# Second layer's output projection: six heads by seven half-size products, the sums of y kept in DRAM

## The chip, the cores and the metric

One core of a Trainium2 chip runs the whole kernel. The metric is device time in microseconds: the median of several executions. One execution was also profiled; its rows give the times of single instructions. TensorE (PE) multiplies matrices into PSUM banks, VectorE (DVE), ScalarE (ACT) and GpSimd (POOL) work elementwise, and SyncE (SP), ACT and POOL issue DMAs. Each engine works through its own queue in order.

## What is computed

A decoder step of two layers over 1024 prompt tokens and 8 x 4 sample tokens, together 1056 columns of width 1024. The first layer is a gated linear recurrent unit, the second HGRN2 with 8 heads of 128. The change lies in the last line of the second layer, `y @ w_out`:

```
def _hgrn_layer(x, g_norm, w_in, lb, o_gain, w_out, S0):
    xn = _rmsnorm(x, g_norm)
    u = (xn @ w_in).astype(jnp.float32)
    q, f, iv, gate = jnp.split(u, 4, axis=-1)
    ...
    o, S_T = _hgrn2_chunked(q, k, v, log_g, S0)
    o = o * lax.rsqrt(jnp.mean(o * o, axis=-1, keepdims=True) + EPS) * o_gain.reshape(H_B, DV_B).astype(jnp.float32)
    y = (o.reshape(Bsz, T, INNER_B) * jax.nn.silu(gate)).astype(x.dtype)
    return x + y @ w_out, S_T.astype(x.dtype)
```

After it comes only the final RMS norm.

## The kernel before

Everything is kept transposed: 128 rows of the model width on the partitions, tokens along the free dimension. A float32 product is three matmuls (`mm3`, L238 to L243): each operand is split into a high half rounded to the engine's float32r and a low half, the rest, and high x high, high x low and low x high are summed in PSUM. A split costs ACT one copy (the high half) and DVE or POOL one subtraction (the low half).

The second layer runs head by head. For heads 1 to 7, the input projection of two of the head's four matrices at once (128 columns of q and f, or of gate and v) is done by seven products of half size in place of eight (the scheme of Strassen and Winograd): `seven` takes two 128x1024 blocks of weights as a 2x2 matrix of 128x512 pieces, and the activations as a 2x2 matrix whose columns are the two halves of the tokens, of HT = 528 each. Combinations of activations are built once (`build`, `build1`; the tiles `t2`, `t3`, `t4`), those of the weights for each head on POOL (`combine`, four operations; the low half of a weight is made by ACT and an accumulating DMA that POOL issues, `low`, L315). A product has numbers 1 to 7; a string such as "126b74b53" gives their order, and each b is a burst: a piece of the recurrence (`burst1` to `burst4`) of the head before or of the same head. Within a product there are two passes of QT = 264 tokens, each into its own PSUM bank; products 2, 3 and 5 share one pair of banks, products 1, 4, 6 and 7 the other.

Head h's y leaves the recurrence in `gated`, which `burst4` of head h + 1 runs: L1328 multiplies it, transposed by TensorE, into the gate that waits in the row `SG`. For heads 0 to 5 the row is then stored to DRAM, `yd`, L310.

The output projection has two parts. For the first K1 = 5 heads, after the last `seven`, chunks of 352 tokens of `yd` are loaded again and split (`splits`, L1594 and L328), and for each of the eight blocks m of 128 output rows and each of three chunks, 5 x 3 matmuls of 352 columns are summed in a bank and added on DVE to x (L1635). The bursts that finish heads 6 and 7 stand between these products (`SPOTS1`). The second part, the late one, takes the last K2 = 3 heads in three chunks of tokens of 424, 376 and 256 (`OUT`): 8 x 9 matmuls each, DVE adds them to x (L1732), ACT squares x (L1734), POOL sums the squares (L1743). The norm of a chunk is worked out while the next chunk's products run: after three blocks the row sums (`summed`, L277), after six the spread of the result over the partitions (`spread`, L1689), then the multiplications of `finish` (L1709 on DVE) and the stores of y.

The order on every engine is not that of the program: `Flow` collects the operations with their dependences and an assumed cost, plans them by list scheduling, back and forth, and issues each engine's queue in the order found. Only the operations marked main keep their order on PE. A DMA is issued in the same way, by SP, ACT or POOL, at a place in that engine's queue.

Of the kernel before, what the change touches and what calls it, by code (L numbers as in the profile page):

```python
# [14 lines left out]
F32 = mybir.dt.float32  # L15
# [4 lines left out]
ALU = mybir.AluOpType  # L20
# [5 lines left out]
K1 = 5  # L26
NMM = 3
HC = 1
FQ0, FQ, GV = "1267b4b35", "12b675b43", "126b74b53"
SPOTS, SPOTS0, SPOTS1 = (6, 9, 0, 2), (2, 5, -1, -1), (1, 5, 9, 13, 17, 20)  # L30
# [179 lines left out]
def tile_trunk(ctx: ExitStack, tc: tile.TileContext, xT, prm, hc, w0, wg, wo0, w1, wo1, s_in,  # L210
# [85 lines left out]
    with ExitStack() as l0:  # L296
# [603 lines left out]
        yd = [nc.dram_tensor(f"yd_{h}", (128, TOK), F32, kind="Internal").ap() for h in range(H - 2)]  # L900
# [32 lines left out]
    with ExitStack() as l1:  # L933
# [8 lines left out]
        ls2 = [fixed(f"land{i}", [128, CH], F32, p1) for i in range(1)]  # L942
# [22 lines left out]
        for o, n, keys in ((at, 1024, ATK), (ad, 256, [("ad",)]), (as2, 64, [("as", 0), ("as", 1)]),  # L965
                           (ab, 288, [("ab",)])):
            pool(0.3 * n, lambda o=o: G.memset(o, 0.0), (), keys, 3)
        dve(9, lambda: V.memset(ssq, 1.0), (), [("ssq", i) for i in range(3)], 3)
# [342 lines left out]
        def gated(h, s, sk):  # L1311
# [257 lines left out]
        yh, yl = (list(o[:4]) for o in (xh, xl))  # L1569
        flat = {k: o.rearrange("p x j t -> p (x j t)") for k, o in TB.items()}  # L1570
        for k in ((2, 0), (3, 0), (4, 0), (4, 1)):
            yh.append(flat[k][:, :TOK])
            yl.append(flat[k][:, TOK:])
        for k in range(H):
            if k < 4:
                olds = [("x", 1, k, x) for x in range(2)] + [("T", 1, i, k, x) for i in range(2) for x in range(2)]
            else:
                n, i = ((2, 0), (3, 0), (4, 0), (4, 1))[k - 4]
                olds = [("T", n, i, j, x) for j in range(4) for x in range(2)]
# [3 lines left out]

        def splits(k, cs, eng):

            for c in cs:
                if k < H - 2:
                    x, xk = next(land)
                    dma(x, yd[k][:, chunk(c)], (("yd", k),), (xk,), 3)
                    xk = (xk,)  # L1590
                else:
                    x, xk = SG[k][:, chunk(c)], ykeys(k % 2, c * CH, CH)
# [4 lines left out]
        def yparts(c):  # L1597
# [223 lines left out]
```

## Time and profile before

| | us |
|---|---|
| median of 3 runs | 1075.94 (1075.3 to 1076.88) |
| the profiled execution's own time | 1074.84 |
| its span in the trace | 1073.1 |
| last product of `seven` done, first of the output projection starts | 942.65 |
| late part starts | 1023.43 |
| last matmul of the late part done, row sums of the last chunk | 1061.02 |

The times of single rows are us from the start of the span. In a row of the timeline stand start, duration, engine, line, operation, written tile <- read tiles, sizes, count, and in brackets idle time of the engine before it with what ended it. A row of windows gives for a stretch its length, then for each engine the busy time and the number of instructions, the granted clock of TensorE as a share of full speed, the share of the DMA engines' time, and GB/s. The count takes in the one or two instructions that began before the stretch. Durations of matmuls overlap (a matmul of 264 columns lasts 0.28 us but the next starts after 0.12 us), so the price of a matmul is the distance from start to start.

### The profile page before, as it was taken

What the parts mean: (1) busy time and instruction counts of PE and PEld (TensorE: products, weight loads), DVE (VectorE), ACT (ScalarE), POOL (GpSimd) and SP (SyncE); (2) the same over time, 40 slices, a digit from 0 to 9 for tenths busy, and PEclk for the clock granted to TensorE, in tenths of its full rate; (3) what the DMA queues carried; (4) which work ended last, traced back from release to release, by engine and by line L of the source; (5) the groups of instructions that cost most, each with busy time, mean ns of one, the idle gap of its engine ahead of it and who ended that gap; (6) DMA issues with size and microseconds to landing.
All of it is one profiled execution on the core that took longest, in us unless ns stands there. A gap on an engine that the chain in (4) does not pass through costs nothing.

```text
span 1073.1 us, 25672 instructions
## 1 busy us (share of the span) xinstructions
PE 1050.9 (98%) x10020; PEld 1023.3 (95%) x10020; DVE 745.6 (69%) x1481; ACT 663.7 (62%) x1493; POOL 504.5 (47%) x536
## 2 busy tenths in 40 slices
PE   9999999999999999999989999999999999999997
PEld 9999999999999999999989998989999999989996
DVE  7999996887987787274887556556565475674446
ACT  6578656867765964243467685858586767652323
POOL 3425353354543547455454454455455464541544
PEclk9999999999999999999989999999999999999999
DMA  9111112124832785373675564746465657555204
GB/s 302 60 28 43 56 48 72 58 60 127 270 104 67 217 258 168 108 242 121 188 200 110 130 140 100 178 93 156 89 151 112 155 112 169 140 161 166 84 1 162
DMA packets 92490, 139.59 MB, mean 130 GB/s; under 512 B 11344, under 2 KB 60496, under 8 KB 92368
## 3 DMA queue, kind: packets, MB, share of 16 engines
q1 hardware_dynamic: 75952, 109.49, 31.8%
q0 software_dynamic: 14112, 25.70, 14.3%
q10 hardware_dynamic: 2304, 2.77, 0.8%
q8 instruction: 78, 1.28, 0.5%
q14 instruction: 44, 0.36, 0.1%
HBM read 77.54 MB, written 29.81 MB: 100 GB/s over the span
## 4 chain that ended last, share of the span: by engine, by line
PE 86%; DVE 9%; DMA 3%; issue 1%; ACT 1%; POOL 0%; POOLq 0%; ACTq 0%; SPq 0%; DVEq 0%
PE mm L241 24%; PE mm L242 24%; PE mm L243 23%; PE hg L1057 2%; PE hg L1166 2%; DMA a<-xn 1%; PE hg L1274 1%; PE hg L572 1%; DVE R L1039 1%; PE hg L1276 1%; PE hg L241 1%; PE hg L242 1%; PE hg L243 1%; PE hg L1220 1%; DVE a L1240 1%
## 5 line engine op out<-in xcount | busy, mean ns | idle before, releaser
L241 PE MATMUL mm<-xh,whi 128*128 128x352 f32 (+1 forms) x1111 | 346.6, 312 | 5.7 <-DVE sg L1510 5.7
L242 PE MATMUL mm<-xl,whi 128*128 128x352 f32 (+1 forms) x1111 | 340.7, 307 | 0.0
L243 PE MATMUL mm<-xh,wlo 128*128 128x352 f32 (+1 forms) x1111 | 340.6, 307 | 0.0
L241 PEld LDWEIGHTS mm<-xh,whi 128*128 128x128 f32 x1111 | 209.0, 188 | 8.3 <-DVE sg L1510 6.8
L242 PEld LDWEIGHTS mm<-xl,whi 128*128 128x128 f32 x1111 | 209.3, 188 | 1.5
L243 PEld LDWEIGHTS mm<-xh,wlo 128*128 128x128 f32 x1111 | 209.1, 188 | 0.0
L328 POOL TENSOR_TENSOR wlo<-wraw,whi 128x512 fp32r<-128x512 f32 (+1 forms) x72 | 96.3, 1347 | 105.7 <-ACT whi L383 97.2
L241 PE MATMUL mm<-t,whi 128*128 128x264 f32 (+1 forms) x354 | 104.0, 294 | 0.0
L243 PE MATMUL mm<-t,wlo 128*128 128x264 f32 (+1 forms) x354 | 101.8, 288 | 2.0 <-DMA wlo<-wraw 2.0
L242 PE MATMUL mm<-t,whi 128*128 128x264 f32 (+1 forms) x354 | 101.9, 288 | 0.0
L504 DVE SCALAR_TENSOR_TENSOR k<-xb,prm_sb,k 128x352 f32<-128x352 f32 (+2 forms) x144 | 90.0, 636 | 11.0 <-ACT k L501 6.3
L315 POOL DMA_DIRECT2D wlo<-wraw x59 | 51.6, 888 | 65.6 <-ACT wlo L314 46.6
L1510 DVE TENSOR_TENSOR k<-mm,k 128x264 f32<-128x264 f32 x72 | 30.7, 430 | 62.2 <-PE mm L243 59.4
L243 PEld LDWEIGHTS mm<-t,wlo 128*128 128x128 f32 x354 | 67.2, 190 | 2.3 <-DMA wlo<-wraw 2.3
L241 PEld LDWEIGHTS mm<-t,whi 128*128 128x128 f32 x354 | 67.5, 191 | 0.5 <-ACT k L1487 0.2
L242 PEld LDWEIGHTS mm<-t,whi 128*128 128x128 f32 x354 | 67.5, 191 | 0.0
L587 POOL TENSOR_TENSOR k<-X 128x352 f32<-128x352 f32 x36 | 42.8, 1198 | 47.8 <-DVE R L588 38.6
L383 ACT CAST whi<-wraw 128x512 fp32r<-128x512 f32 (+2 forms) x75 | 41.3, 569 | 31.3 <-PE mm L242 19.8
L315 POOL DMA_DIRECT2D wlo<-R x36 | 33.5, 929 | 49.7 <-ACT wlo L314 48.2
L241 PE MATMUL mm<-yh,whi 128*128 128x352 f32 x153 | 49.9, 326 | 0.0
L243 PE MATMUL mm<-yh,wlo 128*128 128x352 f32 x153 | 49.4, 323 | 0.0
L242 PE MATMUL mm<-yl,whi 128*128 128x352 f32 x153 | 49.4, 323 | 0.0
(422 smaller groups left out, 2742.1 us busy)
## 6 DMA issues: line engine op xcount, KB each, us to landing
wraw<-in_w_dram SPq DMA_DIRECT2D x88, 256.0 KB, 3.1
wlo<-wraw POOLq DMA_DIRECT2D x59, 256.0 KB, 4.1
wlo<-R POOLq DMA_DIRECT2D x36, 256.0 KB, 4.0
wraw<-in_wo_dram SPq DMA_DIRECT2D x34, 192.0 KB, 2.5
si<-in_s_in_dram SPq DMA_DIRECT2D x8, 512.0 KB, 4.5
R<-in_w_dram SPq DMA_DIRECT2D x16, 256.0 KB, 3.8
out_ss_out_dram<-si SPq DMA_DIRECT2D x8, 512.0 KB, 2.6
sg<-x1b SPq DMA_DIRECT2D x21, 176.0 KB, 3.1
```

What stands on the lines that cost most here:

```text
L241: T.matmul(out, wh, xh, start=first, stop=False, skip_group_check=chained)
L242: T.matmul(out, wh, xl, start=False, stop=False, skip_group_check=chained)
L243: T.matmul(out, wl, xh, start=False, stop=last, skip_group_check=chained)
L315: fl.add("POOL", 0.93, lambda: G.dma_start(dst.bitcast(F32), src, accum_op=ALU.add), (*r, *w), w, prio, n / 2)
L328: emit = lambda: e.tensor_tensor(b, x, a.bitcast(F32), op=ALU.subtract)
L383: act(m, lambda hi=hi, raw=raw, m=m: S.copy(hi[:, :m], raw[:, :m]), rk, (hk,), prio)
L504: dve(u, lambda src=src, dst=dst, sh=sh, k=k: V.scalar_tensor_tensor(dst, sh(src, k), pc("cw", 12 * k + m), dst, op0=ALU.mult, op1=ALU.add ...
L572: fl.add("PE", 0.62, lambda ps=ps, i=i, c=c: T.matmul(ps[:96, :CH], gs[:, i, :], ST[:96, chunk(c)], start=True, stop=True), (("gs",), *((" ...
L587: pool(CH, lambda x=x, a=a, b=b: G.tensor_tensor(x, a.bitcast(F32), b.bitcast(F32), op=ALU.add), (ak, bk), (xk,), 3)
L1057: T.matmul(ps[32 * j:32 * j + 32, n * w:n * w + w], B[:, o:o + 32], q(slice(o, o + 32)), start=True, stop=True, tile_position=(0, 32 * j))
L1166: T.transpose(ps[:, n * 128:(n + 1) * 128], row[:, a:a + 128], ident)
L1510: dve(QT, lambda: V.tensor_tensor(o[0], z[0], u[0], op=ALU.add), (z[1], u[1]), (o[1],), 0)
```

## The change

K1 becomes 6, K2 becomes 2. The first six heads are multiplied by the scheme of seven products, with three heads each as the two rows of the 2x2 matrix: head h and head h + 3 pair up (j = h mod 3), blocks m and m + 1 of the output are the two rows of the weights, the two halves of the tokens the columns. Instead of storing y, `gated` stores what the seven products need of it. `ysum` in DRAM has seven places for each j; a head's two halves are written or added to several of them: for heads 0 to 2 two plain stores (four places at once, then one) and one accumulating store of three places, for heads 3 to 5 two plain stores of one place and accumulating stores of three places and of one. Signs are dealt with by `hogn`, the negative of the gain, for which L1328 is cut at token 528. The accumulating stores are issued by POOL, and each waits until the earlier stores to the same places have landed.

`youts` loads the seven operands (three pieces of 528 tokens each) into the places from which the last `seven` reads its own, as each comes free, and splits them: one piece on DVE, two on POOL. `seven_out` then does the products, for four pairs of blocks: 7 x 2 passes x 3 x 3 matmuls of 264 columns for each pair. Its weights, pieces of 128x384, are combined and their low halves subtracted on POOL, 11 operations for each pair. Each pass is added to x2 by DVE, 264 columns at a time. The orders of products and bursts are in `LAST`. The late part keeps its shape with two heads in place of three.

```diff
-K1 = 5
+K1 = 6
...
-SPOTS, SPOTS0, SPOTS1 = (6, 9, 0, 2), (2, 5, -1, -1), (1, 5, 9, 13, 17, 20)
+SPOTS, SPOTS0 = (6, 9, 0, 2), (2, 5, -1, -1)
+LAST = "12b675b43", "126b74b53", "12b675b43", "1267543"
...
             for ps, pk, a, n in got:
-                w = SG[h][:, a:a + n]
-                dve(n, lambda ps=ps, w=w: V.scalar_tensor_tensor(w, ps, hog[:, h:h + 1], w, op0=ALU.mult, op1=ALU.mult),
-                    (pk,), ykeys(h % 2, a, n), 3)
-            if h < H - 2:
-                dma(yd[h], SG[h], ykeys(h % 2, 0, TOK), (("yd", h),), 4, 528)
+                for u, v in [(0, min(n, HT - a)), (HT - a, n)] if h < K1 and a < HT < a + n else [(0, n)]:
+                    w, z = SG[h][:, a + u:a + v], ps[:, u:v]
+                    by = hogn if h < K1 and (h < 3) == (a + u >= HT) else hog
+                    dve(v - u, lambda z=z, w=w, by=by: V.scalar_tensor_tensor(w, z, by[:, h:h + 1], w, op0=ALU.mult, op1=ALU.mult),
+                        (pk, ("hogn",)), ykeys(h % 2, a + u, v - u), 3)
+            if h < K1:
+                j, first, second = h % 3, (SG[h][:, :HT], ykeys(h % 2, 0, HT)), (SG[h][:, HT:], ykeys(h % 2, HT, HT))
+                for add, (x, xk), a, b in ((False, first, 0, 4), (False, second, 4, 5), (True, second, 1, 4)) if h < 3 else \
+                        ((False, first, 5, 6), (False, second, 6, 7), (True, second, 2, 5), (True, first, 3, 4)):
+                    y, x, keys = ysum[j, :, a:b, :], x[:, None, :].to_broadcast([128, b - a, HT]), [("ysum", p, j) for p in range(a, b)]
+                    if add:
+                        fl.add("POOL", 0.93, lambda y=y, x=x: G.dma_start(y, x, accum_op=ALU.add), (*xk, *keys), keys, 4, 264 * (b - a))
+                    else:
+                        dma(y, x, xk, keys, 4, 264 * (b - a))
...
+        def youts(p):
...
+            for (hi, lo), j, m in pieces:
+                src, sk = ysum[j, :, place_of[p], :], ("ysum", place_of[p], j)
...
+                dma(lo.bitcast(F32), src, (sk,), (lk,), 2, 264)
+                act(HT, lambda hi=hi, lo=lo: S.copy(hi, lo.bitcast(F32)), (lk,), (hk,), 2)
+                subtract(YSUB[j], HT, lo, lo.bitcast(F32), hi, (hk, lk), (lk,), 2)
...
+        YSUB = V, G, G
...
+        def seven_out(m, order, at):
...
+            def split(p):
+                (raw, rk), (hi, hk), (lo, lk) = slot[named[p]], next(his), next(los)
+                hi, lo = hi[:, :u], lo[:, :u]
+                act(u, lambda: S.copy(hi, raw), (rk,), (hk,), 2)
+                subtract(V if p in BYDVE else G, u, lo, raw, hi, (rk, hk), (lk,), 2)
...
+            combine("s", "21", "22", ALU.add)
+            combine("21", "11", "21", ALU.subtract)
+            combine("11", "s", "11", ALU.subtract)
+            combine("12", "11", "12", ALU.subtract)
...
+                for x in range(2):
+                    ps, pk = chains[p in (2, 3, 5)][x]
+                    new = p in (1, 2, 5) or apart and p == 3
+                    ops = [(a[:, x * QT:x * QT + QT], b[:, x * QT:x * QT + QT], k) for a, b, k in youtput[p]]
+
+                    def emit(ps=ps, ops=ops, hi=hi, lo=lo, new=new):
+                        for j, (uh, ul, _) in enumerate(ops):
+                            w = slice(128 * j, 128 * j + 128)
+                            mm3(ps[:, :QT], (hi[:, w], lo[:, w]), uh, ul, new and j == 0, j == 2, True)
+
+                    pe(1.09, emit, (*wk, *(k for o in ops for k in o[2])), (pk,))
...
+                    if p == 1:
+                        add(m, first, z, ALU.add)
...
-        for n, (m, c) in enumerate([(m, c) for c in range(NCH) for m in range(2)] + [(m, c) for m in range(2, KD) for c in range(NCH)]):
...
-            ps, pk = product(ws2[m], yparts(c), 8 if m > 1 else 1)
-            dve(CH, lambda x=x, ps=ps: V.tensor_tensor(x, ps[:, :CH], x, op=ALU.add), (pk, *xk), xk, 0)
+        for i, order in enumerate(LAST):
+            seven_out(2 * i, order, ends_[2 * i:2 * i + 2])
```

The queues move at three places. The first is POOL's where the last of the six heads' y is handed over (during `seven` of head 7). `wlo` is the low half of a weight, `gp` a small copy for the recurrence. Before:

```order
L1437 TENSOR_TENSOR wraw<-wraw,R 128x512
L1437 TENSOR_TENSOR R<-R,wraw 128x512
L315 DMA wlo<-wraw 128x512 x2
L1050 COPY gp<-sg 128x8
L315 DMA wlo<-wraw 128x512
```

and now:

```order
L1449 TENSOR_TENSOR wraw<-wraw,R 128x512
L1341 DMA ysum<-sg 128x3x528
L1449 TENSOR_TENSOR R<-R,wraw 128x512
L317 DMA wlo<-wraw 128x512
L1053 COPY gp<-sg 128x8
L317 DMA wlo<-wraw 128x512
L1341 DMA ysum<-sg 128x528
L317 DMA wlo<-wraw 128x512
```

The accumulating store of three places stands ahead of the weight combination for product 6 and of the low half of that product's weight; the second store stands ahead of product 4's. For heads 3 and 4 it is the same but for the place of `gp`; for heads 0 to 2 the one accumulating store comes behind the low halves of products 6 and 7.

The second place is POOL's queue from the last low halves of `seven` into the output projection (`vb` and `ab` belong to the bursts, `xl` and `t_...` hold y's parts). Before:

```order
L328 TENSOR_TENSOR t_5230<-wraw,t_5230 128x512
L1198 TENSOR_TENSOR vb<-vst,bm 96x512
L328 TENSOR_TENSOR t_5230<-wraw,t_5230 128x128
L328 TENSOR_TENSOR t_5232<-wraw,t_5232 128x512
L328 TENSOR_TENSOR t_5232<-wraw,t_5232 128x128
L1098 COPY ab<-R 128x8x4
L1198 TENSOR_TENSOR vb<-vst,bm 96x512
L328 TENSOR_TENSOR wlo<-wraw,whi 128x512
```

and now:

```order
L1201 TENSOR_TENSOR vb<-vst,bm 96x512
L330 TENSOR_TENSOR xl<-xl,xh 128x528 x2
L330 TENSOR_TENSOR t_5230<-t_5230,t_5229 128x528 x2
L330 TENSOR_TENSOR wlo<-wraw,whi 128x384
L1658 TENSOR_TENSOR R<-wraw 128x384
L1658 TENSOR_TENSOR wraw<-wraw 128x384
L1658 TENSOR_TENSOR wraw<-R,wraw 128x384
L330 TENSOR_TENSOR t_5232<-t_5232,t_5231 128x528 x2
L330 TENSOR_TENSOR wlo<-R,whi 128x384
L330 TENSOR_TENSOR t_5234<-t_5234,t_5233 128x528 x2
L330 TENSOR_TENSOR xl<-xl,xh 128x528
L1101 COPY ab<-R 128x8x4
```

The three subtractions between the first `vb` and `ab` become fourteen operations: nine pieces of y's parts, for products 2, 6, 7, 4 and 5, the low halves of the weights of products 1 and 2, and three combinations of weights.

The third place is DVE's queue at the change from the second to the third late chunk (424, 376 and 256 columns). Before:

```order
L1709 SCALAR_TENSOR_TENSOR a<-a,prm_sb,hg 128x424
L1732 TENSOR_TENSOR sg<-mm,sg 128x376
L1709 SCALAR_TENSOR_TENSOR sg<-sg,prm_sb,hg 128x424
L1732 TENSOR_TENSOR ST<-mm,ST 128x256
L1709 SCALAR_TENSOR_TENSOR sg<-sg,prm_sb,hg 128x424
L1732 TENSOR_TENSOR R<-mm,R 128x256
L1709 SCALAR_TENSOR_TENSOR sg<-sg,prm_sb,hg 128x424
L1732 TENSOR_TENSOR R<-mm,R 128x256
```

and now:

```order
L1818 TENSOR_TENSOR sg<-mm,sg 128x376
L1818 TENSOR_TENSOR ST<-mm,ST 128x256
L1795 SCALAR_TENSOR_TENSOR R<-R,prm_sb,hg 128x424
L1818 TENSOR_TENSOR k<-mm,k 128x256
L1818 TENSOR_TENSOR R<-mm,R 128x256
L1795 SCALAR_TENSOR_TENSOR a<-a,prm_sb,hg 128x424
L1795 SCALAR_TENSOR_TENSOR sg<-sg,prm_sb,hg 128x424 x2
L1761 TENSOR_SCALAR nr_5254<-hg 128x1 x2
```

Of the eight multiplications of the first chunk, five stand behind the first addition of the third chunk, where it was two.

More of the change, by code (lines that the diff above doesn't have):

```diff
@@ L1595, in splits @@
                 subtract(eng, CH, b, x, a, (*xk, ("yh", k, c)), (("yl", k, c),), 1)
-        def yparts(c):
-            return [(yh[k][:, chunk(c)], yl[k][:, chunk(c)], (("yh", k, c), ("yl", k, c))) for k in range(K1)]
-        own = []
-        for i, o in enumerate(ks):
-            key = ("k", i, 1)
-            inherit(key, [("s", j) for j in range(6) if j * QT < (i + 1) * CH and (j + 1) * QT > i * CH])
-            own.append((o[0], key))
-        own.sort(key=lambda o: max(fl.readers.get(o[1]) or [0]))
@@ L1606, in tile_trunk @@
-        land2 = [(o, ("land", i)) for i, o in enumerate(ls2)]
-        land = chain(land2, own[:3], [(t[:, :CH], k) for t, k in rawq if k[0] == "W"], cycle(own))
-        for c in range(NCH):
-            for k in range(K1):
-                splits(k, (c,), V if k % 3 < 2 else G)
-        splits(5, range(NCH), G)
+        x2 = [Gs, KR[:, :TOK], R[:, 2], R[:, 1], Bs, B2, VT, Gc]
+        old = [GK, [("s", i) for i in range(6)], eight("A", 0), eight("A1"), eight("B"), eight("B2"), [("VT", i) for i in range(4)],
+               [("Gc", l) for l in (1, 2, 4, 8, 16, 32)]]
```

146 lines of the change are left out of this document (98 added, 48 removed).

## The prediction

> **What bounds the kernel now.** I read the profile's page first, then the waits of PE in the second layer, then windows over each stage that the change touches.
>
> ```profile
> PE 1050.9 (98%) x10020; PEld 1023.3 (95%) x10020; DVE 745.6 (69%) x1481; ACT 663.7 (62%) x1493; POOL 504.5 (47%) x536
> PE 86%; DVE 9%; DMA 3%; issue 1%; ACT 1%; POOL 0%; POOLq 0%; ACTq 0%; SPq 0%; DVEq 0%
> q0 software_dynamic: 14112, 25.70, 14.3%
> ```
>
> TensorE is busy for 98% of the span and is 86% of the chain that ended last, so a matmul saved is time saved wherever the operands keep pace. That is the question, since the change puts POOL, at 47%, and its DMA queue q0 to more use.
>
> ```profile
> PE mm L241 <- DVE sg L1510: 5.7, 5, 2.2
> PE mm L241 <- ACT xh L1594: 1.0, 1, 1.0
> PE mm L242 <- POOL xl L328: 0.7, 1, 0.7
> ```
>
> These waits of PE (total, times, longest) are nearly all that it loses there: the first where a product of `seven` starts a bank that DVE has just read, the others where y's parts come late for the output projection. The windows (length; PE, PEld, DVE, ACT, POOL; clock, DMA share, GB/s) are:
>
> ```profile
> 942.65:951.81 9.16, 7.16 (x32) 6.35 (x31) 6.20 (x14) 3.52 (x8) 2.69 (x4) 0.81 0.81 255
> 944.00:948.00 4.00, 2.23 (x8) 1.71 (x9) 3.32 (x8) 1.51 (x4) 1.08 (x1) 0.87 0.79 240
> 948.00:952.00 4.00, 4.00 (x20) 4.00 (x20) 1.53 (x3) 1.95 (x4) 0.82 (x1) 0.70 0.88 274
> 951.81:957.55 5.74, 5.74 (x166) 4.94 (x164) 2.74 (x8) 3.04 (x18) 1.34 (x2) 1.00 0.68 202
> 942.65:1023.43 80.78, 78.78 (x680) 75.66 (x678) 42.85 (x96) 27.58 (x90) 30.32 (x32) 0.98 0.40 130
> 1021.04:1023.43 2.39, 2.39 (x17) 2.39 (x16) 0.53 (x1) 0.00 (x0) 0.00 (x0) 1.00 0.00 0
> 1023.43:1037.20 13.77, 13.77 (x73) 13.50 (x73) 4.72 (x8) 3.91 (x7) 5.61 (x6) 1.00 0.01 2
> 1037.20:1051.25 14.05, 14.05 (x84) 13.69 (x83) 7.83 (x20) 4.75 (x9) 8.04 (x8) 1.00 0.09 34
> 1042.97:1047.45 4.48, 4.48 (x27) 4.48 (x27) 2.04 (x8) 1.31 (x3) 3.03 (x4) 1.00 0.00 0
> 1051.25:1061.02 9.77, 9.77 (x81) 9.52 (x81) 7.41 (x19) 5.07 (x12) 5.72 (x7) 1.00 0.40 144
> 1055.21:1058.28 3.07, 3.07 (x28) 3.07 (x28) 1.85 (x7) 1.04 (x3) 2.52 (x4) 1.00 0.22 78
> 913.98:919.82 5.84, 5.84 (x50) 5.84 (x49) 4.95 (x12) 5.40 (x13) 4.70 (x5) 1.00 0.55 92
> ```
>
> Rows of unbroken products give the price of a matmul, once the one or two that began earlier are left out of the count: 264 columns 5.84/48 = 0.122 us, 352 columns 2.39/15 = 0.16, 424 columns 13.77/72 = 0.191, 376 columns 4.48/26 = 0.172, 256 columns 3.07/26 = 0.118. Time goes with columns, so fewer columns is a true gain.
>
> **A, the products: -7.9.** The K1 part goes from 8 x 3 x 15 = 360 matmuls of 352 columns (57.6 us) to 7 x 4 x 2 x 9 = 504 of 264 (61.3 us), +3.7: one head more. Each late chunk goes from 72 to 48 matmuls: 24 x (0.191 + 0.172 + 0.118) = 11.6 off. All of it lies on PE, so it counts in full where PE stays the bound.
>
> **B, the output projection's own waits: -1.4.** The first row above holds 30 matmuls, 4.8 us of work, in 9.16 us: 4.4 lost, of which 1.7 at a reduced clock ((1 - 0.87) x 4 + (1 - 0.70) x 4) and the rest waiting for y's parts and their start. Whether that goes depends on POOL, whose rows are (groups, then the timeline):
>
> ```profile
> L328 POOL TENSOR_TENSOR wlo<-wraw,whi 128x512 fp32r<-128x512 f32 x6 | 7.7, 1290 | 19.7 <-ACT whi L383 19.7
> L1743 POOL TENSOR_TENSOR R<-R,a 128x424 f32<-128x424 f32 x5 | 5.5, 1096 | 10.9 <-ACT a L1734 10.9
> L1743 POOL TENSOR_TENSOR R<-R,a 128x376 f32<-128x376 f32 x5 | 5.0, 996 | 5.1 <-ACT a L1734 5.1
> L1302 POOL TENSOR_TENSOR rst<-rst,mhalf 128x4 f32<-128x4 f32 x4 | 4.5, 1134 | 5.5 <-DVE rst L1300 5.5
> L1198 POOL TENSOR_TENSOR vb<-vst,bm 96x512 fp32r<-96x512 f32 x4 | 4.1, 1037 | 12.3 <-DVE vst L1182 6.3 <-PE hg L1249 6.0
> L1654 POOL TENSOR_TENSOR xl<-wraw,xl 128x384 fp32r<-128x384 f32 x4 | 4.0, 1014 | 2.6 <-ACT xl L1653 2.6
> ```
>
> ```profile
> 929.33 1.04 POOL L1198 TENSOR_TENSOR vb<-vst,bm 96x512 fp32r<-96x512 f32 x1 [2.83 <-DVE vst L1182]
> ```
>
> An operation of 384 takes 1.01 us; one of 528 I put at 1.29 x 528/512 = 1.33, one of 256 at 1.01 x 256/384 = 0.68. From this `vb` on, POOL's new queue reaches the low half of product 2's weight after 1 + 4 x 1.33 + 4 x 1.01 + 2 x 1.33 + 1.01 = 14.1 us, at 943.4. If product 1 starts at 942.65, product 2 is due 18 x 0.122 later, at 944.8: a slack of 1.4, the thinnest of all. Two pieces (946.1) are for products behind the burst; product 6's weight is done by 950.7 and due after a burst like that of 951.81 (5.74 us), at 952.8. Up to 1023.43, 44 operations of weights, 14 of y and 8 late ones make 44.4 + 18.6 + 5.4 = 68.4 us of POOL in 94.1, beside some 10 of the bursts (4.5 + 4.1 and small ones). It fits, without much to spare.
>
> Two things cost anew. A set of sums that starts where DVE still reads the bank waits as in `seven`: 5.7 us there over the 14 sets of seven heads, so 1.6 for four. The start of product 1, whose last operands come free only with the last `seven`, I put at 1.4. Lost 3.0 in place of 4.4. Bounds: 0.5 lost (-3.9), if loads and splits are all early, to 8 (+3.6), if product 2 and a later pair's weights are late and the clock drops as it did.
>
> **C, the late part's tail: +2.0.** The additions on DVE, the squares on ACT and their sums on POOL stay as many, while PE has a third less. First chunk: PE 13.77 - 4.59 = 9.2, POOL 7 x 1.10 = 7.7. Second: PE 14.05 - 4.14 = 9.9, POOL 8.04, DVE 7.83. Third: PE 9.77 - 2.83 = 6.9 against DVE's 7.41. So DVE is the longer there, and five of the first chunk's eight multiplications have moved behind the third chunk's first addition. I take 2.0: 0.5 for the third chunk, 1.5 for an addition or a row sum that comes late. Bounds: 0.5, and 5, if POOL's sums in both earlier chunks run on past their products.
>
> **D, the accumulating stores during `seven`: +3.0.** No row of before shows such a store to DRAM. Nearest are the accumulating low halves, on the same queue:
>
> ```profile
> wlo<-wraw POOLq DMA_DIRECT2D x59, 256.0 KB, 4.1
> ```
>
> q0 moved 25.70 MB in 14.3% of 1073.1 us, 167 GB/s, so 811 KB takes D = 4.9 us. For heads 3 to 5 it is issued right behind a combination of weights and ahead of product 6's low half. The timeline of the two loops:
>
> ```profile
> 855.15 1.56 POOL L1437 TENSOR_TENSOR wraw<-wraw,R 128x512 f32<-128x512 f32 x1
> 858.01 1.77 POOL L1437 TENSOR_TENSOR wraw<-wraw 128x512 f32<-128x512 f32 x1 [1.29 <-ACT ST L1519]
> 859.73 1.77 POOL L315 DMA_DIRECT2D wlo<-wraw  x2
> ```
>
> ```profile
> 909.57 1.84 POOL L1437 TENSOR_TENSOR wraw<-wraw,R 128x512 f32<-128x512 f32 x1 [0.69 <-DMA wlo<-wraw]
> 913.96 1.35 POOL L1437 TENSOR_TENSOR R<-R,wraw 128x512 f32<-128x512 f32 x1 [2.54 <-ACT whi L1429]
> 915.25 1.78 POOL L315 DMA_DIRECT2D wlo<-wraw  x2
> ```
>
> ```profile
> 863.02 0.28 PE L241 MATMUL mm<-t,whi 128*128 128x264 f32 x1
> ...
> 919.82 0.28 PE L241 MATMUL mm<-t,whi 128*128 128x264 f32 x1
> ...
> 928.86 0.39 PE L241 MATMUL mm<-t,whi 128*128 128x264 f32 x1
> ```
>
> In head 6's loop the store can start at 855.15 + 1.56 = 856.7 and the low half is issued 3.0 later; landing 4.1 after that it has no margin for product 6 (863.02), which is late by D - 3.0 = 1.9. In head 7's, from 909.57 + 1.84 = 911.4, the low half follows 3.8 later, lands at 919.3 and is read by the third matmul at 920.1, 0.7 to spare: D - 4.5 = 0.4. Head 5's I put between, nearer the second, at D - 4.2 = 0.7. Together 3D - 11.7 = 3.0. The store's issue itself fits into POOL's idle 1.29 and 2.54. For heads 0 to 2 the store comes behind both low halves: nothing, covered by some 6 us of product and burst before the next is due. Head 5's second store waits until the first has landed (about 918.8); product 4's low half behind it then lands near 925, before product 4 at 928.86. SP's stores grow by one place in seven, its loads come in 21 pieces for 18: covered by a DMA share of 0.40. Bounds of D's term: 0 (a store as quick as a plain one; a gain is excluded, as nothing is taken away there) and 17.7 (D = 9.8, if reading, adding and writing DRAM doubles the time).
>
> The Trainium skill, "DMA: Bandwidth & Descriptors", section "Anatomy of one DMA — SWDGE (gpsimd) path", gives 2.0 us plus bytes over 436 GB/s. By that an estimate for the store is 3.9 us, of which 1.9 on the queue, and the term is 0, the sum -7.3. The trace speaks against it: 256 KB by that rule land after 2.6 us, and here after 4.1.
>
> **Sum:** -7.9 - 1.4 + 2.0 + 3.0 = -4.3. The profiled execution took 1074.84 (span 1073.1, the rest lies around it) and becomes 1070.5; it lies 1.1 under the median of 1075.94, so the median becomes 1071.6.
>
> **Rivals.**
> (1) Nothing is lost: the transition is smooth (-3.9), the tail costs 0.5, D nothing: -11.3, 1064.6. For it, PE's waits are few in before; against it, the slack of 1.4 and the zero margin at 863.02.
> (2) The stores are slow, the slower side: place, product 6 in three loops; price 3D - 11.7. With A to C at -7.3 the kernel is slower by more than 2.15 us once the term passes 9.5, at D = 7.1 us (114 GB/s). At D = 9.8 it is 17.7, and the time 1075.94 - 7.3 + 17.7 = 1086. For it, the store reads DRAM before it adds; against it, q0's 167 GB/s is itself from accumulation.
> (3) POOL bounds the start: if its walk of 14.1 us is a third longer, product 2 waits 3.3, and a clock window adds 1.7; the same for the next pair makes 10 lost for 4.4, +5.6 in place of -1.4: 1078.6. For it, 14 operations where three stood; against it, the bursts between the products.
> (4) The late part is bound by DVE and POOL, and only the first chunk's 4.6 is gained: -0.9 - 1.4 + 3.0 = +0.7, 1076.6. For it, 6.9 against 7.41; against it, PE still has more than POOL in the first two chunks.
>
> **How the numbers follow.** Forecast 0.46, (1) 0.15, (2) 0.14, (3) 0.13, (4) 0.12. The forecast's own range, from half the losses to half as much again, is 1068 to 1075. The whole range is 1065 to 1080: left out are most of (2) and a little of (1). A measurement can tell about 0.2%, 2.15 us. Faster, under 1073.8: 0.41 of the forecast, all of (1), 0.04 of (4), 0.60. Within: 0.04, 0.05 of (3), 0.06 of (4) and 0.02 of (2), 0.17. Slower, over 1078.1: 0.12 of (2), 0.08 of (3), 0.03 else, 0.23.
>
> **What would show it.** A: 264-column products at 0.122 us, late chunks of about 9.2, 9.9 and 7. B: PE waits under 3 us between the last `seven` and the first burst, and granted clock back at 1.00. C: row sums within 2 us of the last product. D: landings of the accumulating stores, 4.9 us of transfer, and waits of product 6 for `wlo` of 1.9, 0.4 and 0.7. The prediction is wrong if product 6 waits over 3 us in those loops, if products 2 or 6 of a later pair wait for POOL, or if the span from the late part's start to the end shrinks by less than 8 us.

## The result, and the profile after

The change takes 1120.57 us (median of 6 runs, 1114.64 to 1123.46), the kernel before 1076.41 in the same runs (1071.39 to 1079.63): a ratio of 1.040, 95% interval 1.037 to 1.044. Forecast were 1071.6, and 1080.0 as the upper end. Slower was given a chance of 0.23.

The profiled execution is the slowest of the six (1123.46). Its span is 1121.7 us, 48.6 more than before, where the medians differ by 44.2. First the page, the lines that answer to those shown of before, and DMA issues (issues, KB of one, median us from issue to landing; 792 KB of 1024 bytes are the 811 KB of the prediction):

```profile
PE 1058.8 (94%) x10092; PEld 1027.9 (92%) x10092; DVE 778.3 (69%) x1515; ACT 675.5 (60%) x1512; POOL 556.9 (50%) x581
...
q0 software_dynamic: 16944, 31.37, 16.8%
...
PE 75%; DVE 10%; DMA 6%; issue 6%; ACT 2%; POOL 2%; POOLq 0%; ACTq 0%; SPq 0%; DVEq 0%
...
ysum<-sg POOLq DMA_DIRECT2D x6, 792.0 KB, 8.1
```

TensorE has only 8 us more work but 49 us more of span, and the chain of waits has 6% of DMA and 6% of "issue", where it had 3% and 1%. The waits of PE in the second layer (total, times, longest) say which DMA:

```profile
PE mm L245 <- DMA wlo<-wraw: 25.2, 7, 6.2
PE mm L245 <- DMA wlo<-R: 9.3, 2, 4.8
PE mm L243 <- DVE sg L1522: 6.3, 6, 2.5
```

Low halves of weights, for which no product waited before after 560 us, now cost 34.5 us. They belong to `seven`, not to the output projection. Windows put a number on each stage (from the first product of `seven`, from the first of the output projection, from the late part, and from its last matmul on). Before:

```profile
535.44:942.65 407.21, 396.72 (x5599) 382.16 (x5592) 254.67 (x563) 286.67 (x718) 203.94 (x203) 0.99 0.60 136
942.65:1023.43 80.78, 78.78 (x680) 75.66 (x678) 42.85 (x96) 27.58 (x90) 30.32 (x32) 0.98 0.40 130
1023.43:1061.02 37.59, 37.59 (x235) 36.70 (x235) 19.96 (x46) 13.74 (x27) 19.37 (x20) 1.00 0.14 51
1061.02:1073.10 12.08, 4.59 (x36) 3.91 (x34) 4.91 (x13) 2.22 (x5) 5.02 (x7) 0.87 0.58 204
```

and after:

```profile
535.24:994.85 459.61, 411.18 (x5600) 394.08 (x5592) 269.72 (x568) 289.48 (x720) 214.95 (x214) 0.95 0.64 145
994.85:1080.22 85.37, 81.14 (x823) 78.08 (x822) 60.47 (x123) 37.40 (x108) 69.04 (x66) 1.00 0.35 115
1080.22:1109.16 28.94, 26.89 (x164) 25.33 (x163) 20.08 (x45) 13.50 (x27) 18.89 (x19) 1.00 0.17 61
1109.16:1121.70 12.54, 5.79 (x36) 4.99 (x34) 5.41 (x14) 1.92 (x5) 5.66 (x7) 0.74 0.59 207
```

| stage | before | after | difference | forecast |
|---|---|---|---|---|
| `seven` | 407.2 | 459.6 | +52.4 | +3.0 |
| output projection, K1 heads | 80.8 | 85.4 | +4.6 | +2.3 (+3.7 - 1.4) |
| late part | 37.6 | 28.9 | -8.7 | -9.6 (-11.6 + 2.0) |
| after the last matmul | 12.1 | 12.5 | +0.5 | 0 |

So the products saved what they were to save, and one term is wrong by 49 us. Where it comes from is seen in one loop, that of head 6. POOL's timeline:

```profile
887.89 0.88 POOL L317 DMA_DIRECT2D wlo<-wraw  x1
888.51 1.58 POOL L1449 TENSOR_TENSOR wraw<-wraw,R 128x512 f32<-128x512 f32 x1
891.54 1.34 POOL L1341 DMA_DIRECT2D ysum<-sg  x1 [1.45 <-ACT ST L1531]
892.40 1.81 POOL L1449 TENSOR_TENSOR wraw<-wraw 128x512 f32<-128x512 f32 x1
900.40 1.81 POOL L317 DMA_DIRECT2D wlo<-wraw  x2 [6.20 <-issue]
```

the landing of that one store (all rows of `ysum` issued from 891 to 892, us from issue to landing):

```profile
DMA to landing us min/median/max: 8.5/8.5/8.5
```

PE's timeline at product 6:

```profile
898.05 0.28 PE L244 MATMUL mm<-t,whi 128*128 128x264 f32 x1
903.85 0.59 PE L245 MATMUL mm<-t,wlo 128*128 128x264 f32 x1 [5.51 <-DMA wlo<-wraw]
```

and the windows of the five products around it, and of those behind the wait:

```profile
886.13:908.16 22.03, 16.52 (x124) 16.17 (x122) 11.77 (x20) 13.03 (x30) 11.13 (x12) 0.85 0.71 136
903.85:908.16 4.31, 4.31 (x23) 4.17 (x23) 0.32 (x1) 1.12 (x3) 1.74 (x2) 0.63 1.07 203
```

After the store is issued, POOL computes one combination and then stands still for 6.2 us with nothing that the profile shows to wait for ("issue"). The next DMA goes out at 900.40, and the store landed at 891.54 + 8.55 = 900.09. The two low halves behind it are issued together, product 6 gets the first at 903.8 and has waited 5.5 us, and then runs at a clock of 0.63 for 4.3 us, which is another 1.6. The stretch takes 22.0 us; before, the same 120 matmuls took 14.8:

```profile
851.21:866.02 14.81, 14.81 (x123) 14.67 (x121) 9.17 (x21) 12.78 (x30) 11.46 (x10) 1.00 0.55 124
```

It is so in all six loops with such a store: behind each store of three places, the next DMA of POOL goes out 0.31 or 0.32 us after the landing, never earlier. In all six, ACT had made the copy for that next low half before the store was issued (by 0.5 to 6.1 us). So where the profile puts POOL's idle time down to an ACT operation that ended just then, as it does in five of the six, that operation was not the cause. The products there are longer by 7.1, 6.4 and 7.3 us in the loops of heads 2 to 4 (product 4 waits) and by 6.6, 7.2 and 8.1 in those of heads 5 to 7 (product 6 waits), 42.7 us in all. In the loops of heads 3 and 4 product 6 also waits ahead of the store, for 2.3 us each with the slow matmuls; that makes 47. The other 5 us of the 52.4 lie in smaller waits of products and bursts and were not followed up.

### The profile page after: what moved, and what is told of

Read it like the earlier page. It is cut to its first block, busy times and chain, and to the rows that moved or that the text cites. A ratio compares the mean times of both kernels' runs of the same rounds, so it can differ in the third digit from the quotient of the medians.

```text
span 1121.7 us, 25970 instructions
## 1 busy us (share of the span) xinstructions
PE 1058.8 (94%) x10092; PEld 1027.9 (92%) x10092; DVE 778.3 (69%) x1515; ACT 675.5 (60%) x1512; POOL 556.9 (50%) x581
## 4 chain that ended last, share of the span: by engine, by line
PE 75%; DVE 10%; DMA 6%; issue 6%; ACT 2%; POOL 2%; POOLq 0%; ACTq 0%; SPq 0%; DVEq 0%
PE mm L243 21%; PE mm L245 21%; PE mm L244 20%; DMA wlo<-wraw 2%; PE hg L1060 1%; DVE R L1042 1%; PE hg L574 1%; PE hg L1277 1%; PE hg L243 1%; PE hg L244 1%; PE hg L245 1%; PE hg L1169 1%; PE hg L1279 1%; DMA a<-xn 1%; DVE t L330 1%
## 5 line engine op out<-in xcount | busy, mean ns | idle before, releaser
L243 PE MATMUL mm<-xh,whi 128*128 128x352 f32 (+1 forms) x1147 | 355.6, 310 | 7.5 <-DVE sg L1522 6.3
L245 PE MATMUL mm<-xh,wlo 128*128 128x352 f32 (+1 forms) x1147 | 349.6, 305 | 0.5 <-POOL wlo L330 0.5
L244 PE MATMUL mm<-xl,whi 128*128 128x352 f32 (+1 forms) x1147 | 349.7, 305 | 0.0
L245 PE MATMUL mm<-t,wlo 128*128 128x264 f32 x408 | 122.5, 300 | 37.7 <-DMA wlo<-wraw 26.9
L330 POOL TENSOR_TENSOR wlo<-wraw,whi 128x512 fp32r<-128x512 f32 (+1 forms) x77 | 104.8, 1369 | 90.8 <-ACT whi L385 75.5
L243 PE MATMUL mm<-t,whi 128*128 128x264 f32 x408 | 123.2, 302 | 0.7 <-ACT k L1499 0.7
L244 PE MATMUL mm<-t,whi 128*128 128x264 f32 x408 | 120.5, 295 | 0.0
L245 PEld LDWEIGHTS mm<-t,wlo 128*128 128x128 f32 x408 | 82.0, 201 | 40.0 <-DMA wlo<-wraw 28.6
L317 POOL DMA_DIRECT2D wlo<-wraw x59 | 53.5, 940 | 83.3 <-ACT wlo L316 45.7
L243 PEld LDWEIGHTS mm<-t,whi 128*128 128x128 f32 x408 | 82.1, 201 | 1.3 <-ACT k L1499 1.0
L244 PEld LDWEIGHTS mm<-t,whi 128*128 128x128 f32 x408 | 82.0, 201 | 0.1
L1064 DVE COPY_PREDICATED attnd<-mask,hg 128x256 f32<-128x256 uint8 x40 | 17.8, 444 | 64.8 <-PE hg L1060 62.0
L1499 ACT COPY k<-mm 128x264 f32<-128x264 f32 x84 | 31.8, 378 | 43.2 <-PE mm L245 42.6
```

The costliest lines, as they stand in the source:

```text
L243: T.matmul(out, wh, xh, start=first, stop=False, skip_group_check=chained)
L244: T.matmul(out, wh, xl, start=False, stop=False, skip_group_check=chained)
L245: T.matmul(out, wl, xh, start=False, stop=last, skip_group_check=chained)
L317: fl.add("POOL", 0.93, lambda: G.dma_start(dst.bitcast(F32), src, accum_op=ALU.add), (*r, *w), w, prio, n / 2)
L330: emit = lambda: e.tensor_tensor(b, x, a.bitcast(F32), op=ALU.subtract)
L1064: dve(256, lambda: V.copy_predicated(ad, MASK[level][:, None, :].to_broadcast([128, 8, 32]), ps), (pk,), (("ad",),), 2)
```

## The experiments

The time of a single run is given with that of a run of the kernel before on the same chip, in brackets; single times of one kernel differ by 4 us and more, stages of a trace by some 2 us. "Stages" are those of the table: `seven`, output projection of the K1 heads, late part.

**No accumulating stores.**

```diff
                     if add:
-                        fl.add("POOL", 0.93, lambda y=y, x=x: G.dma_start(y, x, accum_op=ALU.add), (*xk, *keys), keys, 4, 264 * (b - a))
+                        continue
```

> The accumulating stores are left out: y's sums then lack the added terms, so that the output is not the reference's; all else stays. Theory Q (POOL's own DMA queue takes at most 384 rows that have not landed; a store of three places has 3 x 128 = 384, so that it waits until the queue is empty and the next DMA of POOL waits until it has landed): the six waits of products for a low half, 4.4 to 6.2 us each, go, and the slow matmuls behind them; stretches of seven that grew by 47 us in the profile shrink back, 1121.7 - 47 = 1075 of span, 1071 to 1079. Rival P (the new order of POOL's other work is late by itself): waits for low halves stay, over 1095.

1072.56 (1071.10); stages 411.8, 83.6, 28.2. `seven` is 48 us shorter than in the change, and low halves are hardly late (two waits, 1.5 us in all). That speaks against rival P, but without the stores the planner also finds another order for POOL. The next run keeps the order.

**The same stores, plain.** As above, but `G.dma_start(y, x)`, without the addition.

> The same nine stores by POOL as plain stores, without the addition (the sums lack terms as in the run before). Theory Q: what blocks is the number of rows, not the addition; the next DMA of POOL still goes out 0.3 us after the store has landed. It lands sooner than 8 us if the addition is what slows the transfer: with 5 us each product waits some 3 us less, 1090 to 1112. Rival A (only the reading and adding in DRAM is slow, and a low half behind the store waits because bytes move in order): waits of products for low halves nearly gone, under 1082, and low halves are issued while the store is on its way.

1086.63 (1071.10); stages 418.3, 89.7, 28.9. The order of all operations on POOL, DVE, ACT and SP is that of the change, only the addition is gone, and `seven` is 41 us shorter: rival P falls. Stores of three places landed after 5.6 us in the median (4.0 to 6.5), and low halves did go out while one was under way. POOL's timeline in the loop of head 2:

```profile
628.49 1.80 POOL L317 DMA_DIRECT2D wlo<-wraw  x2
629.63 1.47 POOL L1341 DMA_DIRECT2D ysum<-sg  x1
...
632.33 0.89 POOL L317 DMA_DIRECT2D wlo<-R  x1 [1.03 <-ACT whi L1441]
633.71 0.85 POOL L317 DMA_DIRECT2D wlo<-R  x1 [0.49 <-issue]
```

This store was issued behind two low halves that had not landed, and two more followed before it landed at 636.0. So theory Q as stated, 384 rows of any kind, falls. Rival A was right that low halves go out while the store is under way, but not in its time, under 1082; waits for low halves are 5.1 us and not gone. What is left is a limit on which a plain row weighs less than an accumulating one: 384 plain and 256 accumulating rows are under way together here, whereas 512 accumulating rows never are, in any run. If both kinds share one room, an accumulating row takes more than one and a half times that of a plain one.

**The same stores, plain, by SP.** As above, but `dma(y, x, (*xk, *keys), keys, 4, 264 * (b - a))`.

> The same nine stores as plain stores by SP, not POOL (the sums lack terms). Theory Q: the queue that is blocked is POOL's alone, so waits for low halves go as with no stores: 1071 to 1080. Rival B (5.7 MB more to move is what takes the low halves' place on the 16 DMA engines): waits of 2 us and more stay, over 1085.

1069.71 (1071.10); stages 406.9, 85.4, 28.2. Products of `seven` wait for a low half once, for 0.2 us, though as many bytes are stored: it is POOL's queue that is blocked, not the 16 DMA engines. `seven` takes what it took before.

**Stores of one place each.**

```diff
-                        fl.add("POOL", 0.93, lambda y=y, x=x: G.dma_start(y, x, accum_op=ALU.add), (*xk, *keys), keys, 4, 264 * (b - a))
+                        for p in range(a, b):
+                            y, key = ysum[j, :, p, :], ("ysum", p, j)
+                            fl.add("POOL", 0.93, lambda y=y, x=x[:, 0, :]: G.dma_start(y, x, accum_op=ALU.add), (*xk, key), (key,), 4, 264)
```

> Each accumulating store of three places is cut into three of one place, 128 rows each; the same bytes, the same sums. Theory Q: three of them fill the queue as one of 384 rows did, but the next low half can go as soon as the first of the three has landed, at 4 to 6 us and not at 8: waits of products shrink from 4.4-6.2 to 2-4 us, 1098 to 1115. Rival A (transfer in order): the low half still stands behind all the bytes, 1115 to 1125.

1084.13 (1071.10); stages 420.6, 85.8, 29.0. The same bytes and the same additions, and 39 us of `seven` are back, more than forecast, since the stores go out one by one between the low halves (POOL's timeline in the loop of head 7):

```profile
917.20 1.37 POOL L1343 DMA_DIRECT2D ysum<-sg  x1
921.54 0.87 POOL L1343 DMA_DIRECT2D ysum<-sg  x1 [2.97 <-PE mm L245]
922.87 0.87 POOL L317 DMA_DIRECT2D wlo<-wraw  x1 [0.46 <-ACT sg L1175]
...
926.92 0.87 POOL L1343 DMA_DIRECT2D ysum<-sg  x1 [1.03 <-issue]
...
930.53 0.90 POOL L317 DMA_DIRECT2D wlo<-wraw  x1 [2.55 <-issue]
```

Three DMAs of 128 rows are under way at most; a fourth that is ready goes out 0.31 us after one of them has landed. Rival A, for which the bytes in front of a low half were the price, forecast 1115 or more and misses. Since low halves now also go out between the stores, this run alone does not rule it out; the next one does.

**Rows or bytes.**

```diff
+                        for q in range(0, HT, QT):
-                        fl.add("POOL", 0.93, lambda y=y, x=x: G.dma_start(y, x, accum_op=ALU.add), (*xk, *keys), keys, 4, 264 * (b - a))
+                            fl.add("POOL", 0.93, lambda y=y[:, :, q:q + QT], x=x[:, :, q:q + QT]: G.dma_start(y, x, accum_op=ALU.add),
+                                   (*xk, *keys), keys, 4, 132 * (b - a))
```

> Each accumulating store is cut in two by columns: 264 of each place and partition, so that a store of three places still has 384 rows, of half the bytes (406 KB). The runs before leave two readings of the limit: rows (an accumulating row taking more than one and a half times the room of a plain one, since the plain stores of 384 rows went out with 256 accumulating rows ahead of them), or bytes. By rows each half goes out only when nothing is under way and holds the next DMA until it has landed: 1108 to 1135, as long or longer than the change. By bytes two halves, or a half and two low halves, go side by side: waits of products shrink to 2 us or less, under 1100.

1119.75 (1077.50); stages 456.5, 85.6, 28.9. Half the bytes, and the twelve stores of 384 rows block as the six did: each is issued 0.36 us after the last DMA ahead of it has landed, and the next goes out behind its landing (POOL's timeline in the loop of head 7):

```profile
944.89 1.32 POOL L1342 DMA_DIRECT2D ysum<-sg  x1 [6.57 <-issue]
...
950.77 0.93 POOL L317 DMA_DIRECT2D wlo<-wraw  x1 [1.93 <-ACT R L1538]
...
956.40 1.31 POOL L1342 DMA_DIRECT2D ysum<-sg  x1 [4.71 <-DVE k L1524]
...
966.46 1.81 POOL L317 DMA_DIRECT2D wlo<-wraw  x2 [8.55 <-issue]
```

So the bytes are not what counts. (The second half writes places of the first and has to wait for it in this program; but the first halves, and what stands behind all twelve, are held up too.) A limit on rows, 384 accumulating ones at most, fits every run here: one DMA of three rows in each partition, or three of one. A limit of three DMAs does not: in the run without the addition four were under way at 869.9, one of them a plain store of 128 rows. No DMA of two rows in each partition was tried.

**The planner told of the price.** `fl.add("POOL", 0.93, ...` becomes `fl.add("POOL", 8.5 if b - a > 1 else 0.93, ...`.

> Only the planner's cost of an accumulating store of three places is changed, from 0.93 us of POOL to 8.5, so that it orders the queues as if POOL were held that long. By theory Q the low halves that products wait for are put ahead of the store: of the eight stretches that grew by 47 us half or less remains, 1080 to 1105. Rival E (the row that holds y is written again soon after, so that a later store holds up the gate and the time is lost there): 1110 or more.

1113.49 (1077.50); stages 453.1, 81.7, 28.9. A miss: the time is that of rival E. The waits of PE in the second layer:

```profile
PE mm L245 <- DMA wlo<-wraw: 15.2, 3, 6.7
PE mm L243 <- ACT k L1499: 12.8, 3, 4.4
```

In the loops of heads 5 to 7 the waits for low halves stay; in those of heads 2 to 4 products wait instead for a result that ACT copies late. The mechanism is not rival E's, though. In the loop of head 2 (POOL's row, then ACT's)

```profile
642.01 1.81 POOL L317 DMA_DIRECT2D wlo<-R  x2 [6.39 <-issue]
645.14 0.63 ACT L316 ACTIVATE wlo<-wraw 128x512 fp32r<-128x512 f32 x1 [5.38 <-POOL wraw L1449]
```

the store, issued at 634.30, landed at 641.70, and POOL went on 0.31 us later. A combination of weights stood behind its two DMAs, ACT's queue waited 5.4 us for it, and the copy for which product 4 waits stood in that queue. The loops of heads 3 and 4 show the same, with 5.1 us each. It is still POOL's blocked queue, now by way of ACT; this order did not hide the eight microseconds.

**Fewer accumulating rows.**

```diff
+                if h < 3:
+                    put(0, f, fk)
+                    put(4, s, sk)
+                    both(s, sk)
+                    put(1, s, sk, 3)
+                else:
+                    put(5, f, fk)
+                    put(6, s, sk)
+                    more(2, s, sk)
+                    more(4, s, sk)
+                    both(f, fk)
+                    more(3, f, fk)
```

Here `f` and `s` are the two halves of y in its row, `put` is a plain store by SP, `both` a sum of the halves by DVE in place, `more` an accumulating store of one place.

> The same seven sums with fewer accumulating rows: for heads 0 to 2 DVE adds the two halves of y in place once the second is stored, and SP stores the sum to its three places; for heads 3 to 5 three accumulating stores of one place each, the third of a sum made by DVE. 9 stores of 128 rows by POOL in place of 6 of 384 and 3 of 128. Theory Q: the loops of heads 0 to 2 lose nothing, those of 3 to 5 at most a short wait: 1068 to 1079, near the run without these stores (1072.6) or with them on SP (1069.7). Rival E (six more operations of DVE, 0.7 us each, and stores that must land before a sum is made hold up the gate's row): over 1085.

1077.84 (1077.50); stages 416.0, 83.5, 29.2. The time is as forecast by theory Q, and up to the end of head 6's loop `seven` is within 3 us of before. In head 7's loop 8 us are lost, more than the short wait that was forecast: a product waits 1.9 us for a low half and a burst 3.2 for DVE.

**Low halves of the first output weights by DMA.** On top of it, `low(u, lo, raw, (rk,), (lk,), 2)` in place of `subtract` for m = 0 in `seven_out`.

> As the run before, and the low halves of the first two blocks' weights in the output projection are made by ACT and accumulating DMAs of POOL, as in seven, not by subtractions on POOL (7 of 384 columns, about 1 us each). If POOL is what is late there (products waited 0.5 us for a low half, a burst 0.5 for vb), the first 20 us of the output projection shorten by 1 to 3 us: 1066 to 1077. If DVE is what is late there (the longest wait, 1.7 us, is for DVE), it is the same within 1 us.

1085.71 (1077.50); stages 418.3, 89.9, 28.9. A miss of both: the output projection is 6.4 us longer. Two products wait there, 2.6 us for a low half by DMA and 3.6 for a sum by DVE.

**No accumulating stores, the same sums.** For heads 3 to 5 the earlier sum is loaded into a new tile `yt` of 528 columns, added to and stored again; for heads 0 to 2 it is as in the run before the last.

```diff
+                else:
+                    get(1)
+                    put(5, f, fk)
+                    put(6, s, sk)
+                    plus_(yt, (("yt",),), s, sk)
+                    put(2, yt, (("yt",),))
+                    plus_(f, fk, yt, (("yt",),))
+                    put(3, f, fk)
+                    get(4)
+                    plus_(yt, (("yt",),), s, sk)
+                    put(4, yt, (("yt",),))
```

With `plus_` on DVE:

> The same seven sums with no accumulating store at all: DVE adds, SP stores and loads the earlier sum again (two loads of 264 KB for each of heads 3 to 5), 12 additions of 528 columns on DVE. Theory Q: POOL's queue holds what it held before the change, no product of seven waits for a low half over 1 us, and what is left is the output projection's own balance: 1064 to 1074, ratio 0.99 to 1.00. Rival E (DVE and the gate's row are what is short): over 1078, with waits of bursts and products for DVE.

With `plus_` on POOL:

> As the run before, with the 12 additions on POOL (about 1.3 us each, 16 us of POOL in all). Theory Q: as the run before, 1064 to 1076. If POOL's computing, not only its DMA queue, is short in seven, low halves are late again by 1 us and more in heads 1 to 7: over 1078.

In three rounds, ratios to before of 1.001 (0.999 to 1.003) and 1.000 (0.998 to 1.003), at medians of 1075.5 and 1073.9 (1072.9); stages 411.1, 83.3, 28.9 and 409.8, 85.7, 29.0. The first is above its forecast, and one product of its `seven` still waits 2.3 us for a low half; the second is within. The loss of the change is gone with its stores, in a kernel that computes the same. But it is not faster than before.

**Why not faster: the start of the output projection.** Three runs from the version with `plus_` on DVE: the first burst later (`LAST` begins with "1267b5b43"), `YSUB = G, G, G`, and `YSUB = V, V, G`.

> From the version without accumulating stores and with additions on DVE (span 1070.3, output projection of six heads 83.3 us from its first product to the first late one, of which 61.3 are products and 18.3 bursts where these are not held up): the first burst in the first two blocks stands behind products 6 and 7, not ahead of them. If DVE and POOL are what is late there (both busy for 99% of 950 to 965), two products more ahead of the burst give them 4.4 us: the 83.3 becomes 80.5 to 82.5. If it is the chain of the recurrence itself, the wait moves with the burst: 83 or more.

> From the same version: the 7 subtractions of y's parts that DVE had (528 columns, 0.7 us each) go to POOL (1.3 us each). If DVE is the late one at the start of the output projection, its 83.3 us becomes 81 to 82.5; if POOL is, 85 to 88. Forecast of the prediction's own step B, where POOL had 1.4 us to spare and DVE was not counted: POOL, so longer.

> From the version without accumulating stores (output projection of six heads 83.3 us; 90.6 with DVE's seven subtractions moved to POOL): seven of POOL's fourteen subtractions of y's parts go to DVE instead. If POOL is the engine that is late there, products wait less for it: 81 to 83. If DVE is as short as POOL, bursts wait longer for DVE and it is 84 or more.

1081.07 and 1083.95 (1073.82), 1080.05 (1076.68). The output projection takes 87.1, 90.6 and 89.3 us where it was 83.3. The first settles nothing: the planner's new order also made a burst of `seven` wait 4.3 us. The other two say more, though each is a single run whose queues were planned anew, so that its `seven` is longer too (416.2 and 412.9). The first 15 us of the output projection (windows, in this order: `plus_` on DVE, subtractions moved to POOL, subtractions moved to DVE; under the last two the waits of PE for the engine that is full there: total, times, longest):

```profile
946.60:961.60 15.00, 14.18 (x233) 13.29 (x232) 13.84 (x26) 10.89 (x36) 14.21 (x13) 1.00 0.50 160
```

```profile
951.27:966.27 15.00, 8.43 (x51) 8.22 (x50) 5.67 (x9) 7.84 (x16) 14.80 (x14) 0.77 0.32 109
PE mm L245 <- POOL wlo L330: 7.0, 2, 6.6
```

```profile
948.63:963.63 15.00, 9.72 (x89) 8.51 (x91) 14.96 (x18) 8.44 (x29) 10.93 (x10) 0.97 0.39 114
PE hg L1253 <- DVE si L1260: 3.5, 1, 3.5
```

In the first, DVE (13.8) and POOL (14.2) are both nearly full (over 950 to 965 it is 14.7 and 14.3, so 98% and 95% and not the 99% of the expectation). With more on POOL, POOL is (14.8) and DVE is not (5.7); PE works 8.4 of 15 us, and a product waits 6.6 us for a low half that POOL subtracts. With more on DVE, DVE is (15.0); PE works 9.7, and a burst waits 3.5 us for DVE. Neither has room for the other's work there, and moving it costs 6 to 7 us either way.

**Head 5's additions on POOL, the rest on DVE.** One run, then five rounds of the same kernel.

> From the same version: the three additions for head 5, in the loop that runs into the output projection, are on POOL, the nine others on DVE. If DVE's additions there are what holds up the burst at 934 (1.7 us) and with it the start of the output projection, the loops take 407 to 409.5 us and not 411.1; if POOL is as short there, 411 or more.

> The version of the run before, timed in rounds against the kernel before, to see whether the scheme gains once no accumulating store is in POOL's queue. By the stages of the profiles (seven +0.4, output projection +6.9, late part -8.7, rest -0.6) it is 2 us shorter: ratio 0.998, 0.996 to 1.000. If the profile was a lucky execution: 1.000 to 1.003 as the two versions before.

1072.87 (1076.68), then a ratio of 1.0005 (0.9986 to 1.0024) in rounds. The loops do shorten, to 407.6, but the output projection takes 87.7; the second profile has 409.5 and 86.7. The difference of 2 us was one execution's. No version that makes the whole sums beats the kernel before.

## Why the prediction was wrong

**A, the products, was right.** The late part's windows are 8.7 us shorter; forecast with its tail were 9.6. A matmul of 264 columns took 0.122 us as forecast (162 in 19.81 us at the end of the output projection).

**D, the accumulating stores, is the step that failed: +52.4 in `seven` for +3.0.** It held that the store takes 4.9 us of transfer on q0, that the low half behind it is issued 3.0 or 3.8 us later all the same, and that only the transfer stands in its way. Three things in it were wrong.
- The price. 8.1 us in the median from issue to landing. As plain stores the same bytes took 5.6 by POOL and 5.1 by SP, so the addition is some 2.5 of it. The bound of 9.8 held for the transfer.
- The overlap. The prediction asked how long a low half travels behind the store; it is not issued at all until the store has landed. That is why the sum 3D - 11.7 is too small even with the measured 8.1 (12.6 us, where the three products lost 21.9): its 11.7 us are head starts, and there were none. With the waits come the slow matmuls, 1.6 us behind the one shown.
- Heads 0 to 2, costed at nothing because the store comes behind the low halves of 6 and 7. Product 4's stands behind it, and the 6 us of cover are less than 8.1 + 0.3 + 3.4 (the landing of a low half issued at once). The stretches behind these three stores lost 20.8 us.

The Trainium skill, "DMA: Bandwidth & Descriptors", section "Anatomy of one DMA — SWDGE (gpsimd) path", gave an estimate of 3.9 us for this store. Measured were 8.1, and 5.6 without the addition (4.0 the shortest), so the measurement decides here.

Rival (2) had the right side and the right place for heads 3 to 5, but as a slow transfer, at 1086. It was given 0.14.

**B, the output projection's waits: its number was near by luck, and a term was missing.** Forecast were 3.0 us lost among the products; measured are 85.4 - 61.3 - 20.7 = 3.4, where 20.7 are the bursts. The parts are others. Sets of sums that wait for DVE, put at 1.6, cost 0.15, and no wait for the start of product 1, put at 1.4, is seen; instead a matmul that reads a low half, at 1009.0, came 1.4 late, with no cause that the profile names. Product 2 of the first pair waited 0.46 us for its low half, so the walk along POOL's queue, with 1.4 to spare, was off by some 2. But the bursts were taken as unchanged at 18.3, and they take 2.4 us more. The windows of the first two bursts and the products between them, before and after:

```profile
951.81:969.80 17.99, 17.99 (x287) 16.85 (x285) 13.37 (x27) 8.94 (x33) 8.21 (x8) 1.00 0.34 110
```

```profile
999.98:1019.01 19.03, 15.41 (x280) 13.98 (x279) 18.33 (x27) 9.75 (x34) 18.95 (x17) 1.00 0.29 91
```

Only POOL's work was added up there, not that of DVE, which has seven subtractions and the additions to x2 beside the bursts' own work. The second window shows both nearly full, DVE for 18.3 and POOL for 18.95 of 19.0 us.

**C, the tail of the late part, was about right:** 28.9 us for 37.6 - 11.6 = 26.0 of products and what stands between them, so 2.9 lost for 2.0.

**The sum without D** was -7.3, and the plain stores by SP, where D is nothing, show -5.1 in span (1067.94 for 1073.06): the bursts' 2.4 are about the difference. In the versions that make the whole sums without accumulating stores, leaving aside the three that change the start of the output projection, `seven` is 0.4 to 4 us longer than before and the output projection 2.5 to 7, and the 8.7 of the late part are used up.

## What to carry to other kernels

A DMA of an in-order engine is priced by what it holds up behind it, not by its bytes: ask first whether the next one can be issued while it is under way. Work out an accumulating store's rows (pieces times partitions) and keep them few, or let the vector engines add and plain stores of another queue carry the sums. And where work is moved to one idle engine, add up every engine that shares the stretch; here POOL was walked and DVE was not.

## What the runs showed of the hardware that was not expected

- POOL's DMA queue behaves here as if it had room for a number of rows. In no run were more than 384 accumulating rows (128 to 384 to a DMA) under way at once. A store of 384 is issued 0.35 us after all ahead of it has landed, and the next DMA 0.31 us after it has landed; with accumulating DMAs of 128 rows a fourth waits until one of three has landed. Halving the bytes of a row changes nothing (12 stores out of 12); plain rows weigh less (384 plain and 256 accumulating together). While it waits POOL is idle; the profile calls it "issue", or names another engine's operation that happened to end then.
- Adding in DRAM, in medians of six: 8.1 us to landing for 811 KB by accumulating stores, 5.6 by plain ones of the same queue, 5.1 by plain ones of SP.
- A wait of PE of 5.5 us was followed by 4.3 us at a mean clock of 0.63. What the exact size of the room is, and how much more an accumulating row takes than a plain one, was not tried.
